# The last 64 places of a diagonal prefix sum: from one row of sums to 64 partitions under bf16 weights

## The chip, the cores and the metric

The kernel runs on one core of one Trainium2 chip. The metric is the device time of one execution in microseconds (us), taken several times; the median counts. Beside it there is a profile of one execution, whose own times are counted from its first instruction. Its engines are TensorE (PE, with the weight loads as PEld), VectorE (DVE), ScalarE (ACT), GpSimd (POOL) and SyncE (SP). SP does no arithmetic here, it only starts transfers.

## The reference

```python
def setup_inputs():
    B, H, W = 4, 4224, 4224
    return {"x": np.random.randn(B, H, W).astype(np.float32)}

def reference(x):
    ps = np.cumsum(np.cumsum(x, axis=1), axis=2)
    diag = np.diagonal(ps, axis1=1, axis2=2)
    return np.cumsum(diag, axis=1).astype(np.float32)
```

For each of four 4224 x 4224 matrices (batches), the two-dimensional prefix sum is taken along its diagonal, and the diagonal is summed up once more. The output has 4 x 4224 float32 numbers; the input has 285 MB, and every element of it is read.

## The kernel before

The places of the diagonal lie in 11 groups of 384. For each batch, strips of 768 rows are loaded (converted to bf16 by the load). TensorE counts column sums per group, VectorE and ScalarE count row sums, and two scans in VectorE turn the 11 x 384 sums into the output. The last batch (`b == 3`, not `whole`) is arranged so that little is left to do once its last rows have come in: rows 3840 to 4223 form the last group, and its last 128 rows come as four blocks of 32 rows. A block of 32 rows of 4096 columns lies on all 128 partitions, four partitions to a row, 1024 columns each; `part_b[:, s]` is block `s`. A row contributes to a place by how many places lie from that row's own place up to it, which is what the weights hold: `weights4[p, j]` counts this for partition `p` (row `p // 4` of a block) and place `j` counted from the block's first place.

The tail, which the change touches (cuts are marked `...`):

```python
    R = P // 4                                   # 32 rows of a block; P = 128
    steps = consts.tile([P, P], I32, name="steps")
    nc.gpsimd.iota(steps, pattern=[[4, P]], base=7, channel_multiplier=-1)
    ...
    weights4 = consts.tile([P, P], FP32, name="weights4")
    nc.vector.tensor_scalar_max(out=weights4, in0=steps, scalar1=0.0)
    ...
    M0 = 2 * P                                   # 256
    E0 = GW - R                                  # 384 - 32 = 352
    ...
        if not whole:
            fin_a = psum_s.tile([1, M0], FP32, name="fin_a")
            fin_b = psum_s.tile([1, P], FP32, name="fin_b")
            fin_e = psum_s.tile([1, R], FP32, name="fin_e")

        def weigh_b(rows, w, r0=0, start=False):
            matmul(fin_b[:, r0:], rows, w[..., : P - r0], start=start)
    ...
            CB = TB // 4                         # 1024 columns to a partition
            bcut = 768
            for sb, c0, c1 in ((0, 0, CB), (1, 0, CB), (2, 0, CB), (3, 0, bcut), (3, bcut, CB)):
                r0 = TB + sb * R
                nc.gpsimd.dma_start(
                    out=part_b[:, sb, c0:c1],
                    in_=x[b, r0 : r0 + R, :TB].rearrange("r (k c) -> r k c", k=4)[:, :, c0:c1],
                )
    ...
        for c in range(0, CB, P):                # block 0
            matmul(by_ps, part_b[:, 0, c : c + P], weights4_h, start=c == 0)
        ...
        act_sum(bsum[:, 0, 0:1], part_b[:, 1, :512])           # block 1: two halves
        pair_sum(bsum[:, 0, 1:2], part_b[:, 1, 512:])
        for i in (1, 0):
            weigh_b(bsum[:, 0, i : i + 1], weights4, R)
        nc.vector.tensor_add(out=yl[:, :M0], in0=fin_a, in1=last_sums[0:1, :M0])
        nc.sync.dma_start(out=out[b, T0 : T0 + M0].unsqueeze(0), in_=yl[:, :M0])
        nc.sync.dma_start(out=out[:LB, :].rearrange("b (g i) -> g b i", i=GW), in_=whole_sums)
        nc.sync.dma_start(out=out[b, :T0].rearrange("(g i) -> g i", i=GW), in_=last_sums[1:NG])
        act_sum(bsum[:, 1, 0:1], part_b[:, 2, :448])           # block 2
        pair_sum(bsum[:, 1, 1:2], part_b[:, 2, 448:])
        for i in (1, 0):
            weigh_b(bsum[:, 1, i : i + 1], weights4, 2 * R)

        act_sum(esum[:, 0:1], part_b[:, 3, :320])              # block 3
        pair_sum(esum[:, 1:2], part_b[:, 3, 320:bcut])
        pair_sum(esum[:, 2:3], part_b[:, 3, bcut:])
        nc.scalar.copy(out=yl[:, M0:], in_=fin_b)
        nc.sync.dma_start(out=out[b, T0 + M0 : T0 + E0].unsqueeze(0), in_=yl[:, M0:E0])
        for k in (1, 0, 2):
            matmul(fin_e, esum[:, k : k + 1], weights4[:, :R], start=k == 1)
        nc.vector.tensor_add(out=ye, in0=fin_e, in1=yl[:, E0:])
        nc.sync.dma_start(out=out[b, T0 + E0 : N].unsqueeze(0), in_=ye)
```

`act_sum` is a row sum on ScalarE, `pair_sum` one on VectorE that adds two halves of its input and sums the result. `matmul` loads its weights (`lhsT`) and streams `rhs`; `matmul_on` streams under the weights that are in place. Each engine runs its instructions in the order of the program, and SP too.

Of the kernel before, what the change touches and what calls it, by code (L numbers as in the profile page):

```python
# [8 lines left out]
FP32 = mybir.dt.float32  # L9
BF16 = mybir.dt.bfloat16  # L10
I32 = mybir.dt.int32
AX = mybir.AxisListType
# [5 lines left out]
def kernel(  # L18
# [14 lines left out]
    nc = tc.nc  # L33

    B, H, W = x.shape
    N = H
    P = 128
    F = 3
    F2 = 2 * F
    GW = P * F  # L40
# [3 lines left out]
    T0 = LG * GW  # L44
# [4 lines left out]
    consts = ctx.enter_context(tc.tile_pool(name="consts", bufs=1))  # L49
# [4 lines left out]
    last = ctx.enter_context(tc.tile_pool(name="last", bufs=1))  # L54
# [3 lines left out]
    psum_s = ctx.enter_context(  # L58
        tc.tile_pool(name="psum_s", bufs=1, space=bass.MemoryType.PSUM)
    )  # L60
# [61 lines left out]
    for i in range(1, NBUF):  # L122
# [5 lines left out]
        out=um1,  # L128
        in_=um1,
        compare_op=ALU.is_gt,  # L130
        fill=0.0,
        base=0,
        pattern=[[1, GW]],
        channel_multiplier=-1,
# [5 lines left out]
        out=ident,  # L140
        in_=ident,
        compare_op=ALU.is_equal,
        fill=0.0,
        base=0,
        pattern=[[-1, P]],
        channel_multiplier=1,
# [27 lines left out]
    def between_groups(name, turned):  # L174
# [27 lines left out]
        out=weights,  # L202
        in_=weights,
        compare_op=ALU.is_ge,
        fill=0.0,
        base=0,
        pattern=[[1, GW]],
        channel_multiplier=-1,
# [1 line left out]


    R = P // 4
    steps = consts.tile([P, P], I32, name="steps")
    nc.gpsimd.iota(steps, pattern=[[4, P]], base=7, channel_multiplier=-1)
    nc.vector.tensor_single_scalar(
        out=steps, in_=steps, scalar=2, op=ALU.arith_shift_right
    )
    weights4 = consts.tile([P, P], FP32, name="weights4")
    nc.vector.tensor_scalar_max(out=weights4, in0=steps, scalar1=0.0)

    ident_h = consts.tile([P, P], BF16, name="ident_h")
    nc.vector.tensor_copy(out=ident_h, in_=ident)
# [1 line left out]
    def matmul(o, lhsT, rhs, start=False):  # L224
        nc.tensor.matmul(  # L225
            o, lhsT=lhsT, rhs=rhs, start=start, stop=False, skip_group_check=True
        )

    def matmul_on(o, lhsT, rhs):

        te = nc.tensor
        te.add_instruction(  # L232
            mybir.InstMatmult(
                start_tensor_calc=False,
                stop_tensor_calc=False,
                tile_position=(0, 0),
                tile_size=(P, P if lhsT.shape[-1] > 64 else 32),
                bass_skip_group_check=True,
                ldweights=False,
                name=nc.get_next_instruction_name(),  # L240
                engine=te.engine,
                ins=[
                    te.lower_ap(rhs, opt=False),
                    te.lower_ap(lhsT, opt=False, for_matmul_weights=True),
                ],
                outs=[te.lower_ap(o)],
            )
        )

    weights4_h = consts.tile([P, P], BF16, name="weights4_h")  # L250
    nc.vector.tensor_copy(out=weights4_h, in_=weights4)
    ones_col = consts.tile([P, 1], FP32, name="ones_col")
    nc.vector.memset(ones_col, 1.0)

    def fold_in(o, src, c0, c1, w, start=False):

        for c in range(c0, c1, w):
            e = min(c + w, c1)
            if c == c0:
                matmul(o[..., : e - c], ident_h, src[..., c:e], start=start)  # L260
            else:
                matmul_on(o[..., : e - c], ident_h, src[..., c:e])

    def act_sum(acc, src):
        w = src.shape[-1]
        dump = dumpool.tile([P, 2176], BF16, name="dump")
        nc.scalar.activation(  # L267
            out=dump[:, :w], in_=src, func=ACT.Copy, accum_out=acc
        )
# [6 lines left out]
    def pair_sum(acc, src):  # L276

        w = src.shape[-1] // 2
        if not pairs:
            pairs.append(last.tile([P, 288], FP32, name="pair"))  # L280
        pair = pairs[0]
        nc.vector.scalar_tensor_tensor(
            out=pair[:, :w],
            in0=src[:, :w],
            scalar=1.0,
            in1=src[:, w:],
            op0=ALU.mult,
            op1=ALU.add,
            accum_out=acc,
        )  # L290
# [37 lines left out]
    last_sums = last.tile([NG, GW], FP32, name="last_sums")  # L328

    M0 = 2 * P  # L330
    E0 = GW - R

    for b in range(B):
        whole = b < LB
# [9 lines left out]
        def row_of(j):  # L344
            return (j + t0) % NG

        if not whole:
            fin_a = psum_s.tile([1, M0], FP32, name="fin_a")
            fin_b = psum_s.tile([1, P], FP32, name="fin_b")
            fin_e = psum_s.tile([1, R], FP32, name="fin_e")  # L350

        def weigh_b(rows, w, r0=0, start=False):

            matmul(fin_b[:, r0:], rows, w[..., : P - r0], start=start)
# [8 lines left out]
        def columns(j, lo, hi, rhs, same=False):  # L363


            k = row_of(j)
            lhsT = sel[:, NG - 1 - k : 2 * NG - 1 - k]
            if same:
                matmul_on(d[:, lo:hi], lhsT, rhs)
                return  # L370
            matmul(d[:, lo:hi], lhsT, rhs, start=first[0])
            first[0] = False
# [65 lines left out]
        for h in range(2):  # L438
            ps = slice(h * HP, (h + 1) * HP)
            k = row_of(h)  # L440
            nc.vector.tensor_copy(
                out=r6[ps, k : k + 2 * ns : 2, :], in_=a6[ps, :, :, 1]
# [24 lines left out]
        if not whole:  # L467
# [3 lines left out]
            part_b = strip[:, 2, :TB].rearrange("p (s c) -> p s c", s=4)  # L471
# [3 lines left out]
            CB = TB // 4  # L475
            bcut = 768
            for sb, c0, c1 in (
# [8 lines left out]
                    out=part_b[:, sb, c0:c1],  # L486
                    in_=x[b, r0 : r0 + R, :TB].rearrange("r (k c) -> r k c", k=4)[
                        :, :, c0:c1
                    ],
# [29 lines left out]
        for i, (to, src) in enumerate(((c1, d), (c2, c1))):  # L519
            nc.vector.tensor_tensor_scan(  # L520
                out=to,
# [8 lines left out]


        yl = last.tile([1, GW], FP32, name="yl")
        ye = last.tile([1, R], FP32, name="ye")
        c0, c1 = acuts[1]
        fold_in(fold_a, part_a, c0, c1, 256)
        by_ps = psum_s.tile([P, P], FP32, name="fold")
# [9 lines left out]


        bsum = last.tile([P, 2, 2], FP32, name="bsum")
        esum = last.tile([P, 3], FP32, name="esum")
        act_sum(bsum[:, 0, 0:1], part_b[:, 1, :512])  # L550
        pair_sum(bsum[:, 0, 1:2], part_b[:, 1, 512:])
        for i in (1, 0):
            weigh_b(bsum[:, 0, i : i + 1], weights4, R)
        nc.vector.tensor_add(out=yl[:, :M0], in0=fin_a, in1=last_sums[0:1, :M0])
        nc.sync.dma_start(
            out=out[b, T0 : T0 + M0].unsqueeze(0), in_=yl[:, :M0]
        )
        nc.sync.dma_start(
            out=out[:LB, :].rearrange("b (g i) -> g b i", i=GW), in_=whole_sums
        )  # L560
        nc.sync.dma_start(
            out=out[b, :T0].rearrange("(g i) -> g i", i=GW), in_=last_sums[1:NG]
        )
        act_sum(bsum[:, 1, 0:1], part_b[:, 2, :448])
        pair_sum(bsum[:, 1, 1:2], part_b[:, 2, 448:])
        for i in (1, 0):
            weigh_b(bsum[:, 1, i : i + 1], weights4, 2 * R)


        act_sum(esum[:, 0:1], part_b[:, 3, :320])  # L570
        pair_sum(esum[:, 1:2], part_b[:, 3, 320:bcut])
        pair_sum(esum[:, 2:3], part_b[:, 3, bcut:])
        nc.scalar.copy(out=yl[:, M0:], in_=fin_b)
        nc.sync.dma_start(
            out=out[b, T0 + M0 : T0 + E0].unsqueeze(0), in_=yl[:, M0:E0]
        )
        for k in (1, 0, 2):
            matmul(fin_e, esum[:, k : k + 1], weights4[:, :R], start=k == 1)
        nc.vector.tensor_add(out=ye, in0=fin_e, in1=yl[:, E0:])
        nc.sync.dma_start(out=out[b, T0 + E0 : N].unsqueeze(0), in_=ye)  # L580


# [28 lines left out]
```

## Time and profile before

| what | value |
|---|---|
| median of 3 runs | 667.94 us (667.25 to 668.96) |
| profiled execution: time, span | 667.23 us, 665.5 us |
| VectorE busy | 380.3 us, 57% of the span |
| TensorE busy | 206.7 us, 31% |
| ScalarE busy | 136.8 us, 21% |
| DMA | 143.23 MB written, mean 215 GB/s |
| HBM read over the span | 285.47 MB, 429 GB/s |

The span is the time from the first to the last instruction; the rest of the measured time lies outside it. Busy shares are averages over the whole span; the change sits in the last 5 us or so, so the timeline and the waits of that stretch say more than the shares. In a timeline line the columns are start, duration, engine, line of the program, operation, output and inputs with their shapes, count, and in brackets the idle time before it with what ended it. A stretch of fp32 matmuls is counted in passes: one fp32 matmul shows as two.

### The profile page before, as it was taken

What the parts mean: (1) busy time and instruction counts of PE and PEld (TensorE: products, weight loads), DVE (VectorE), ACT (ScalarE), POOL (GpSimd) and SP (SyncE); (2) the same over time, 40 slices, a digit from 0 to 9 for tenths busy, and PEclk for the clock granted to TensorE, in tenths of its full rate; (3) what the DMA queues carried; (4) which work ended last, traced back from release to release, by engine and by line L of the source; (5) the groups of instructions that cost most, each with busy time, mean ns of one, the idle gap of its engine ahead of it and who ended that gap; (6) DMA issues with size and microseconds to landing.
All of it is one profiled execution on the core that took longest, in us unless ns stands there. A gap on an engine that the chain in (4) does not pass through costs nothing.

```text
span 665.5 us, 2519 instructions
## 1 busy us (share of the span) xinstructions
PE 206.7 (31%) x956; PEld 94.5 (14%) x956; DVE 380.3 (57%) x174; ACT 136.8 (21%) x223; POOL 31.7 (5%) x60
## 2 busy tenths in 40 slices
PE   0071522302117143140311723404021354450428
PEld 0030211100003021010000311201000121220103
DVE  4161828476946173756794526557589433362866
ACT  0001120406300103040630020304063002030434
POOL 4300000000000000000000000000000000001000
PEclk9995857656559585665655857657565595875758
DMA  9999999999999999999999999999999999999998
GB/s 203 219 219 219 219 218 218 215 207 216 219 221 218 218 220 217 218 215 210 216 219 220 216 219 218 219 216 214 215 216 218 217 218 218 218 216 219 214 207 165
DMA packets 7666, 143.23 MB, mean 215 GB/s; under 512 B 698, under 2 KB 998, under 8 KB 2150
## 3 DMA queue, kind: packets, MB, share of 16 engines
q0 software_dynamic: 7312, 142.47, 100.0%
q1 hardware_dynamic: 342, 0.61, 0.4%
q8 instruction: 7, 0.11, 0.1%
q14 instruction: 5, 0.04, 0.0%
HBM read 285.47 MB, written 0.07 MB: 429 GB/s over the span
## 4 chain that ended last, share of the span: by engine, by line
DVE 50%; another core or an unknown queue 32%; DMA 15%; POOL 1%; PE 1%; issue 1%; DVEq 0%; POOLq 0%
DVE acc L272 26%; DMA strip<-in_x_dram 14%; DVE rowed L272 7%; DVE mu L387 7%; DVE strip L388 7%; PE d L225 1%; POOL um L107 1%; DMA head<-in_x_dram 1%; DVE um L106 1%; DVE c L520 0%; DVE whole_sums L520 0%; POOL strip L485 0%; DVE pu L272 0%; DVE whole_sums L293 0%
## 5 line engine op out<-in xcount | busy, mean ns | idle before, releaser
L267 ACT ACTIVATE dump<-strip 128x416 bf16<-128x416 bf16 (+6 forms) x108 | 124.4, 1152 | 519.7 <-DMA strip<-in_x_dram 517.0
L387 DVE TENSOR_TENSOR mu<-strip,um 128x4608 bf16<-128x4608 bf16 (+1 forms) x24 | 52.4, 2184 | 254.9 <-DMA strip<-in_x_dram 254.8
L272 DVE TENSOR_REDUCE acc<-strip 128x6 f32<-128x4608 bf16 (+6 forms) x23 | 195.9, 8519 | 0.4
L232 PEld LDWEIGHTS <-sel 128*11 128x11 bf16 x643 | 66.4, 103 | 475.8 <-issue 446.5
L225 PE MATMUL d<-strip,sel 128*11 128x384 bf16 x90 | 37.1, 412 | 280.5 <-DMA strip<-in_x_dram 280.5
L232 PE MATMUL d<-strip,sel 128*11 128x384 bf16 x441 | 116.0, 406 | 13.9 <-DMA strip<-in_x_dram 13.9
L388 DVE TENSOR_TENSOR strip<-strip,mu 128x4608 bf16<-128x4608 bf16 (+1 forms) x24 | 52.4, 2183 | 1.0
L225 PE MATMUL d<-mu,sel 128*11 128x384 bf16 x43 | 16.3, 379 | 108.4 <-DVE mu L387 108.4
L272 DVE TENSOR_REDUCE rowed<-strip 128x384 f32<-128x2304 bf16 x12 | 48.9, 4074 | 0.0
L232 PE MATMUL d<-mu,sel 128*11 128x384 bf16 x200 | 46.3, 366 | 0.0
L76 POOL DMA_DIRECT2D strip<-in_x_dram x23 | 15.6, 680 | 535.3 <-DVE acc L272 293.2
L267 ACT ACTIVATION_READ_ACCUMULATOR dump<-strip 128x1 f32 x108 | 20.1, 186 | 0.0
L225 PE MATMUL d<-rowed,sel_f 128*11 128x384 f32 x24 | 11.7, 576 | 20.9 <-DVE rowed L272 20.9
L225 PEld LDWEIGHTS <-sel 128*11 128x11 bf16 x134 | 13.6, 101 | 23.2 <-issue 11.2
L225 PE MATMUL d<-ident,rows 128*11 128x128 f32 x24 | 5.2, 379 | 16.8 <-DVE rows L450 16.8
L272 DVE TENSOR_REDUCE pu<-d 11x1 f32<-11x384 f32 x4 | 2.2, 546 | 6.2 <-PE d L225 6.2
L107 POOL TENSOR_SCALAR_AFFINE_SELECT um<-um 128x4608 bf16<-128x4608 bf16 (+1 forms) x2 | 5.2, 2622 | 8.7 <-DVE um L106 8.7
L106 DVE MEMSET um<- 128x4608 bf16 (+1 forms) x2 | 4.9, 2458 | 1.1 <-issue 1.1
L225 PE MATMUL d<-halves,rows 128*11 128x64 f32 x48 | 5.3, 289 | 0.0
L225 PEld LDWEIGHTS d<-ident,rows 128*11 128x11 f32 x24 | 2.5, 119 | 18.9 <-DVE rows L450 11.7
L225 PEld LDWEIGHTS d<-rowed,sel_f 128*11 128x11 f32 x24 | 1.5, 92 | 25.4 <-DVE rowed L272 25.1
L225 PEld LDWEIGHTS d<-halves,rows 128*11 128x11 f32 x48 | 4.8, 129 | 1.3 <-issue 1.1
(110 smaller groups left out, 64.6 us busy)
## 6 DMA issues: line engine op xcount, KB each, us to landing
strip<-in_x_dram POOLq DMA_DIRECT2D x18, 6336.0 KB, 72.8
strip<-in_x_dram POOLq DMA_DIRECT2D x7, 3168.0 KB, 55.8
strip<-in_x_dram POOLq DMA_DIRECT2D x1, 1080.0 KB, 49.9
strip<-in_x_dram POOLq DMA_DIRECT2D x1, 768.0 KB, 52.9
strip<-in_x_dram POOLq DMA_DIRECT2D x3, 256.0 KB, 54.1
head<-in_x_dram SPq DMA_DIRECT2D x1, 528.0 KB, 3.9
strip<-in_x_dram POOLq DMA_DIRECT2D x1, 192.0 KB, 43.2
strip<-in_x_dram POOLq DMA_DIRECT2D x1, 64.0 KB, 28.6
```

What stands on the lines that cost most here:

```text
L76: nc.gpsimd.dma_start(out=o, in_=x[b, r0 : r0 + f * P, :].rearrange("(p f) w -> p f w", f=f))
L106: nc.vector.memset(um, 1.0)
L107: nc.gpsimd.affine_select(out=um, in_=um, compare_op=ALU.is_gt, fill=0.0, base=0, pattern=[[-1, f], [1, f * P]], channel_multiplier=-f,)
L225: nc.tensor.matmul(o, lhsT=lhsT, rhs=rhs, start=start, stop=False, skip_group_check=True)
L232: te.add_instruction(mybir.InstMatmult(start_tensor_calc=False, stop_tensor_calc=False, tile_position=(0, 0), tile_size=(P, P if lhsT.shap ...
L267: nc.scalar.activation(out=dump[:, :w], in_=src, func=ACT.Copy, accum_out=acc)
L272: nc.vector.reduce_sum(out=acc, in_=src, axis=AX.X)
L387: nc.vector.tensor_mul(out=mu, in0=block, in1=um)
L388: nc.vector.tensor_sub(out=block, in0=block, in1=mu)
```

## The change

It widens the last piece from 32 to 64 places and turns it onto partitions. Before, block 3 is summed along its columns by ScalarE and VectorE, and the sums are then weighted by TensorE into a row of 32 places on one partition. After, TensorE streams block 3 itself, in eight pieces of 128 columns, under bf16 weights (64 of them per partition, one per place) into a PSUM tile of 64 partitions x 128 columns; VectorE then sums along the columns, so that the sum over columns comes after the weights and in one instruction. Column 129 of that tile holds what the 64 places get from elsewhere: the rows up to block 1 (turned from a row onto partitions by a matmul with a single one), and block 2. The weights get 32 more columns in front, in which block 3 counts nothing for block 2's places. The first 320 places leave in one store instead of two, and the last 64 in a store whose 64 pieces have 4 bytes each, one from each partition. It is meant to shorten the work between the landing of the last rows and the last store.

```diff
-    steps = consts.tile([P, P], I32, name="steps")
-    nc.gpsimd.iota(steps, pattern=[[4, P]], base=7, channel_multiplier=-1)
+    steps = consts.tile([P, R + P], I32, name="steps")
+    nc.gpsimd.iota(steps, pattern=[[4, R + P]], base=7 - 4 * R, channel_multiplier=-1)
 ...
-    weights4 = consts.tile([P, P], FP32, name="weights4")
-    nc.vector.tensor_scalar_max(out=weights4, in0=steps, scalar1=0.0)
+    weights4_w = consts.tile([P, R + P], FP32, name="weights4_w")
+    nc.vector.tensor_scalar_max(out=weights4_w, in0=steps, scalar1=0.0)
+    weights4 = weights4_w[:, R:]
 ...
-    weights4_h = consts.tile([P, P], BF16, name="weights4_h")
-    nc.vector.tensor_copy(out=weights4_h, in_=weights4)
+    weights4_hw = consts.tile([P, R + P], BF16, name="weights4_hw")
+    nc.vector.tensor_copy(out=weights4_hw, in_=weights4_w)
+    weights4_h = weights4_hw[:, R:]
 ...
-    E0 = GW - R
+    S = 2 * R
+    E0 = GW - S
 ...
-            fin_e = psum_s.tile([1, R], FP32, name="fin_e")
+            fin_e = psum_s.tile([S, P + 1], FP32, name="fin_e")
 ...
-        ye = last.tile([1, R], FP32, name="ye")
+        ye = last.tile([S, 1], FP32, name="ye")
 ...
         nc.vector.tensor_add(out=yl[:, :M0], in0=fin_a, in1=last_sums[0:1, :M0])
         nc.sync.dma_start(
-            out=out[b, T0 : T0 + M0].unsqueeze(0), in_=yl[:, :M0]
-        )
-        nc.sync.dma_start(
             out=out[:LB, :].rearrange("b (g i) -> g b i", i=GW), in_=whole_sums
         )
 ...
         act_sum(bsum[:, 1, 0:1], part_b[:, 2, :448])
         pair_sum(bsum[:, 1, 1:2], part_b[:, 2, 448:])
+        nc.vector.tensor_copy(out=yl[:, M0:], in_=fin_b)
+        nc.sync.dma_start(
+            out=out[b, T0 : T0 + E0].unsqueeze(0), in_=yl[:, :E0]
+        )
+
+        matmul(fin_e[:, P:], yl[:, E0:], ones_col[0:1], start=True)
         for i in (1, 0):
-            weigh_b(bsum[:, 1, i : i + 1], weights4, 2 * R)
-
-        act_sum(esum[:, 0:1], part_b[:, 3, :320])
-        pair_sum(esum[:, 1:2], part_b[:, 3, 320:bcut])
-        pair_sum(esum[:, 2:3], part_b[:, 3, bcut:])
-        nc.scalar.copy(out=yl[:, M0:], in_=fin_b)
-        nc.sync.dma_start(
-            out=out[b, T0 + M0 : T0 + E0].unsqueeze(0), in_=yl[:, M0:E0]
-        )
-        for k in (1, 0, 2):
-            matmul(fin_e, esum[:, k : k + 1], weights4[:, :R], start=k == 1)
-        nc.vector.tensor_add(out=ye, in0=fin_e, in1=yl[:, E0:])
-        nc.sync.dma_start(out=out[b, T0 + E0 : N].unsqueeze(0), in_=ye)
+            matmul(fin_e[:, P:], weights4[:, :S], bsum[:, 1, i : i + 1])
+        for c in range(0, CB, P):
+            piece = part_b[:, 3, c : c + P]
+            if c == 0:
+                matmul(fin_e[:, :P], weights4_hw[:, :S], piece, start=True)
+            else:
+                matmul_on(fin_e[:, :P], weights4_hw[:, :S], piece)
+        nc.vector.reduce_sum(out=ye, in_=fin_e, axis=AX.X)
+        nc.sync.dma_start(out=out[b, T0 + E0 : N].unsqueeze(1), in_=ye)
```

More of the change, by code (lines that the diff above doesn't have):

```diff
@@ L236, in matmul_on @@
                 tile_position=(0, 0),
-                tile_size=(P, P if lhsT.shape[-1] > 64 else 32),
+                tile_size=(P, P if lhsT.shape[-1] > 64 else 64 if lhsT.shape[-1] > 32 else 32),
                 bass_skip_group_check=True,
@@ L548 @@
         bsum = last.tile([P, 2, 2], FP32, name="bsum")
-        esum = last.tile([P, 3], FP32, name="esum")
         act_sum(bsum[:, 0, 0:1], part_b[:, 1, :512])
```

## The prediction

> **What bounds the kernel now.** I read the page first, for what fills the span, then the chain that ended last, then the timeline of the last 4 us, and then what SP waits for. On the page, the DMA row shows the 16 DMA engines busy in every slice, and the queue of the loads alone fills them:
>
> ```profile
> DMA  9999999999999999999999999999999999999998
> ...
> q0 software_dynamic: 7312, 142.47, 100.0%
> q1 hardware_dynamic: 342, 0.61, 0.4%
> ```
>
> So the loads set some 662 of the 665.5 us, and nothing in the change makes them fewer. What can move is the tail behind them, and anything that gets in among them. The chain, in order of time (start, duration, what):
>
> ```profile
> 618.94 43.22 DMA strip<-in_x_dram
> ...
> 662.25 0.29 DVE pair L282
> ...
> 662.71 0.57 PE fin_e L225 x6
> ...
> 663.36 0.18 DVE ye L579
> ```
>
> The loads end it until 662.16, then VectorE, TensorE and VectorE follow. The trace's completion records tell the landings apart: block 1 at 659.99, block 2 at 661.22, the first 768 columns of block 3 at 662.16, its last 256 at 662.50 (a transfer is whole at its sixteenth completion). The timeline around them:
>
> ```profile
> 661.32 0.46 DVE L282 SCALAR_TENSOR_TENSOR pair<-strip 128x288 f32<-128x288 bf16 x1
> 661.32 0.98 PE L225 MATMUL fin_b<-weights,bsum 128*1 128x96 f32 x8
> ...
> 662.68 0.29 DVE L282 SCALAR_TENSOR_TENSOR pair<-strip 128x128 f32<-128x128 bf16 x1
> ...
> 662.71 0.55 PE L225 MATMUL fin_e<-weights,esum 128*1 128x32 f32 x6 [0.40 <-DVE pair L282]
> ...
> 663.36 0.18 DVE L579 TENSOR_TENSOR ye<-fin_e,yl 1x32 f32<-1x32 f32 x1 [0.38 <-PE fin_e L225]
> 663.57 0.23 SPq L580 DMA_DIRECT2D out_dram<-ye  x1
> ```
>
> From the last landing (662.50) to the last store's issue (663.57) pass 1.07 us: that is all the arithmetic that the change can shorten. Its packet starts at 664.27, its completion comes at 664.60, 1.03 us after issue, and 0.9 us of closing follow. The last view is SP's waits:
>
> ```profile
> SPq L555 <- DVE yl L554: 660.0, 1, 660.0
> ```
>
> SP starts the head's load at 0.82 us and then stands for 660 us before the first store of `yl`. The two big stores behind it (`whole_sums` 49.5 KB, `last_sums` 15.0 KB) have long been ready: they wait only for SP's order.
>
> **What the Trainium skill says.** "TensorE: Matmul & The Clock Gate", section "LDWEIGHTS (loading the stationary operand)", lets a weight load's time grow with its columns, columns / 1.2 ns: 53 ns for 64, an estimate. No weight load before has 64 columns; those of one column take 79 to 84 ns each, overlapped. "VectorE: DVE Perf Modes", section "The perf-mode tier table (the rule you actually need)", says a reduce handles one element per cycle whatever the type; the trace agrees (11x384 fp32 from PSUM in 546 ns, 128x480 in 650 ns: 1.08 ns a column). "DMA: Bandwidth & Descriptors", section "Issuing engines are not separate DMA queues", says that transfers of all issuing engines share the same 16 DMA engines and interleave, and section "Why a DMA increments its semaphore by 16 and not by 1" that the size of the slowest dimension sets how many engines a store uses. The trace agrees: the `whole_sums` store of 11 partitions completes in 11 steps after a first jump, that of `last_sums` with 10 in 10.
>
> **The change part by part.**
>
> *Removed.* On ScalarE 0.47 + 0.19 us for block 3 and the 0.24 us copy, on VectorE the two sums of block 3 (0.39 + 0.08 and 0.29 + 0.08), on TensorE six passes of 32 columns, and the first `yl` store. On the path are one VectorE sum, TensorE and the add.
>
> *The new chain on TensorE.* In program order, the matmuls over block 3 now stand behind a matmul that needs `yl`, so behind VectorE's copy of `fin_b`. VectorE is done with block 2 at 661.79 (accumulator read 661.70 + 0.08), and the last of the four block-1 passes into `fin_b` starts at 661.57 and takes 0.246, so 661.82. With 0.07 us for the signal the copy starts at 661.89. Its length from two VectorE instructions on one partition, 1x256 in 0.412 and 1x32 in 0.179, is 1.04 ns a column, so 0.28 for 128: done at 662.17, TensorE goes on at about 662.20. Then six fp32 passes with 64-column weights and one streamed column; at about 0.06 us each (the 53 ns above, and a little) 0.36: 662.56. By then both parts of block 3 are there. The eight bf16 matmuls of 128 columns are those of block 0, which took 0.62 us in all (658.77 to 659.39; the granted clock is 1.00 from 655 on). With 0.05 for the first weights they end at 663.23. VectorE starts 0.10 later (before: 663.26 to 663.36), and the reduce of 129 columns takes 0.546 - 255 x 0.00108 = 0.27: 663.60. With 0.03 to SP the store is issued at 663.63, against 663.57 before: +0.06.
>
> If the fp32 passes go faster than this, the landing at 662.50 binds instead: two matmuls behind it (0.05 + 0.06 + 0.22) end at 662.83, and 0.10 + 0.27 + 0.03 put the issue at 663.23, -0.34. That needs TensorE to be through 3a by 662.55, so to be free of the fp32 passes at 662.2, which I believe only in part. I take -0.05.
>
> *The store in 64 pieces.* One piece before: 0.70 us from issue to its packet, then 0.33 to completion. The head's load with its 256 pieces shows its first packet 1.07 us after issue, so (1.07 - 0.70) / 255 = 1.5 ns a piece, 0.09 for 64. Four pieces and a completion on each of 16 engines, at some 20 ns each (the 384-byte packet of `yl` took 20), add 0.08, and the slowest of sixteen engines counts instead of one. I put +0.2 on it.
>
> *Stores that move.* With the first `yl` store gone, SP comes to `whole_sums` at once and issues it when its third scan is done (the scan starts at 520.2 and takes 1.0), and `last_sums` after its second scan at 659.66. Both then run in the middle of a full load stream, where before they ran after it, in the shadow of the tail (their last completion 663.93). 64.5 KB of 1024 bytes are 66 kB; at the 429 GB/s of the page that is 0.15 us, which delays the last landing and everything behind it. At the 215 GB/s of the written side it would be 0.31. I take +0.15.
>
> *At the start* the weights are 160 columns wide instead of 128; three strips of loads are in the queue then, nothing waits for it: 0.
>
> Sum: -0.05 + 0.2 + 0.15 = +0.3 us, the span 665.8 instead of 665.5. On the median of 667.94 that is 668.2 us.
>
> **The rivals.** (a) *TensorE gets through early*, and the chain ends 0.34 earlier; with stores that cost nothing the time is 667.6. For it speaks that the one-column passes are short and the array's clock is full; against it, that two VectorE-to-TensorE handovers stand in its way at 661.8 to 662.2. (b) *The 4-byte pieces are dear*: all 64 land within 256 bytes of HBM, and if their writes go one after another at, say, 20 ns each, the store is 1.3 us longer and the time 669.3. Nothing before has such a store; the completions of 4 bytes (9 ns each) go to semaphores, and prove nothing for HBM. (c) *The moved stores cost nothing or twice as much*: they use 11 and 10 of 16 engines, and only the engines that finish last count. The sixteen completions of the last load spread from 661.17 to 662.50, six of them within 0.1 us of the end, so it can be 0 or 0.3: 668.1 or 668.4.
>
> **Range and chances.** All of these lie within about -0.4 to +1.5 us of the old time. The three runs before spread by 1.7 us, which is more than my step; so the range is mainly that scatter around 668.2: 667.2 to 669.2. Two per cent are 13 us, over four times the 3.0 us from the last landing to the end of the span; nothing here reaches it. Chances: faster by over 2% 0.005, within 2% 0.99, slower by over 2% 0.005.
>
> **What would show it.** `whole_sums` should be issued near 521 us and `last_sums` near 659.7. The copy into `yl` should end before 662.2, the six fp32 passes near 662.6, the reduce take 0.27, and the last store be issued at about 663.6 after a landing at about 662.65. From that issue to its completion should pass 1.2 us. I am wrong if the weight loads of 64 fp32 columns take far from 0.06 us each, if the store of 64 pieces completes in under 1.1 or over 1.6 us, or if the last landing moves by over half a microsecond.

## The result

The changed kernel takes 674.08 us (median of 5 runs, 673.45 to 674.89) against 667.78 us before (5 runs, 667.25 to 668.96). The ratio is 1.009, with a 95% interval of 1.0075 to 1.0105: slower by 6.3 us. The prediction put it at 668.2 us with a range of 667.2 to 669.2. That nothing here would reach two per cent holds, but by luck: it was argued from the 3.0 us between the last landing and the end of the span, and these have become 9.55 us (663.60 to 673.15). The loss is twenty times the step that was predicted, and lies outside the range.

The page of the profile after, with the DMA row and the queues:

```profile
DMA  9999999999999999999999999999999999999993
...
q0 software_dynamic: 7312, 142.47, 98.8%
q1 hardware_dynamic: 418, 0.61, 0.3%
```

The loads are the same packets. The last digit of the DMA row has gone from 8 to 3, and the small queue has 76 packets more: at the end there is a stretch without traffic. What SP waits for, in the profile after (engine, line, what it waited for, us in total, times, longest):

```profile
SPq L557 <- DVE acc L411: 520.5, 1, 520.5
...
SPq L607 <- DMA out_dram<-ye: 6.0, 1, 6.0
SPq L566 <- DVE yl L565: 2.2, 1, 2.2
```

and the last of these in the profile before:

```profile
SPq L606 <- DMA out_dram<-ye: 0.3, 1, 0.3
```

That is the loss. At the end of the program SP waits 6.0 us for the last store, where it waited 0.3. The first line shows that `whole_sums` is no longer held up until 661 us: SP comes to it at once and stands only until its scan is done (the scan ends at 521.65, the store is issued at 521.69; `acc` is what VectorE writes right behind it). The tail's timeline after the change (start, duration, engine, line, operation; idle time before it in brackets):

```profile
663.48 0.28 DVE L565 COPY yl<-fin_b 1x128 f32<-1x128 f32 x1 [0.20 <-PE fin_b L226]
...
663.82 0.27 PE L226 MATMUL fin_e<-ones_col,yl 1*64 1x1 f32 x2 [0.37 <-DVE yl L565]
...
664.02 0.39 PE L226 MATMUL fin_e<-bsum,weights_w 128*64 128x1 f32 x4
...
664.33 0.55 PE L233 MATMUL fin_e<-strip,weights_hw 128*64 128x128 bf16 x7
664.92 0.28 DVE L580 TENSOR_REDUCE ye<-fin_e 64x1 f32<-64x129 f32 x1 [1.16 <-PE fin_e L233]
665.23 0.54 SPq L581 DMA_DIRECT2D out_dram<-ye  x1
```

The new arithmetic is short, as planned, but it starts late: from the last landing (663.60) to the issue pass 1.63 us, where it was 1.07. After the issue at 665.23 nothing computes any more; the table of stretches (length, busy time of PE, PEld, DVE, ACT and POOL with counts, clock, DMA share, GB/s) says so in one line:

```profile
666.00:673.20 7.20, 0.00 (x0) 0.00 (x0) 0.00 (x0) 0.00 (x0) 0.00 (x0) 0.73 0.01 0
```

By the trace's records, the 64 packets of 4 bytes and their sixteen completions have all left the DMA engines by 1.36 us after the issue, each in 7 to 9 ns. But the completions arrive in a staircase from 2.07 to 7.01 us after it. Before, the one packet of 128 bytes was complete after 1.03 us. The two profiled executions lie 7.66 us apart (674.89 and 667.23 us; the profiled one was the longest of the five after). Of these the store accounts for 5.98, the later landing (663.60 instead of 662.50) for 1.10, and the way from landing to issue for 0.56. What it is about this store that costs so much was open.

### The profile page after: what moved, and what is told of

The parts are those of the page before. It is cut to its first block, busy times and chain, and to the rows that moved or that the text cites. A ratio compares the mean times of both kernels' runs of the same rounds, so it can differ in the third digit from the quotient of the medians.

```text
span 673.2 us, 2516 instructions
## 1 busy us (share of the span) xinstructions
PE 207.6 (31%) x960; PEld 95.9 (14%) x960; DVE 379.8 (56%) x171; ACT 136.2 (20%) x220; POOL 31.7 (5%) x60
## 4 chain that ended last, share of the span: by engine, by line
DVE 52%; another core or an unknown queue 34%; DMA 8%; PE 3%; issue 1%; POOL 1%; DVEq 0%
DVE acc L274 27%; DMA strip<-in_x_dram 7%; DVE mu L390 7%; DVE strip L391 7%; DVE rowed L274 7%; PE d L226 1%; DVE c L523 1%; POOL um L107 1%; DMA head<-in_x_dram 1%; DVE um L106 1%; DVE whole_sums L523 0%; PE fold L233 0%; PE d L233 0%; DVE pu L274 0%
```

## The experiments

Theories. **Sharing**: writes of 4 bytes wait for each other because they fall into the same few bytes of HBM. **Pieces**: a small piece, or a descriptor, costs this much wherever it lands. **Source**: 64 partitions or sixteen engines on the SBUF side cost it. **Moved stores** and **chain**: the loss comes from the stores that now run among the loads, or from the new arithmetic, and the late completion is only where it shows. Times of a run are compared with the kernel before on the same chip.

### The 64 numbers in one piece

```diff
         nc.vector.reduce_sum(out=ye, in_=fin_e, axis=AX.X)
-        nc.sync.dma_start(out=out[b, T0 + E0 : N].unsqueeze(1), in_=ye)
+        matmul(fin_r, ye, ident[:S, :S], start=True)     # back onto one partition
+        nc.vector.tensor_copy(out=yr, in_=fin_r)
+        nc.sync.dma_start(out=out[b, T0 + E0 : N].unsqueeze(0), in_=yr)
```

> The changed kernel, but its 64 sums are turned back onto one partition by a matmul with the identity and a copy, and leave in one piece of 256 bytes. If the store of 64 pieces is the cost (7.0 us from issue to completion in the profile after, against 1.0 before), the store's completion comes about 1.0 us after its issue, some 0.6 us are added for matmul and copy, and the time is 674.1 - 6.0 + 0.6 = 668.7 us, within 1.5 us of the kernel before. If the moved stores or the new chain on TensorE are the cost, it stays at 672 to 675 us.

Measured: 668.22 us, before 667.32; ratio 1.0015 (1.0008 to 1.0022). Its store completes 1.06 us after issue. Its tail:

```profile
663.70 0.28 DVE L580 TENSOR_REDUCE ye<-fin_e 64x1 f32<-64x129 f32 x1 [1.16 <-PE fin_e L233]
664.03 0.27 PE L226 MATMUL fin_a<-ident,ye 64*1 64x64 f32 x2 [0.38 <-DVE ye L580]
664.34 0.21 DVE L584 COPY yr<-fin_a 1x64 f32<-1x64 f32 x1 [0.36 <-PE fin_a L226]
664.58 0.23 SPq L585 DMA_DIRECT2D out_dram<-yr  x1
```

From the end of the reduce (663.98) to the issue, the way back takes 0.60 us. With all the rest of the change in place, its moved stores and its chain, 0.90 us of the 6.30 remain, and 0.60 of these are the way back. The loss is the form of the last store; chain and moved stores together can hold only a few tenths.

### The first store of `yl` back in its place

```diff
+        nc.sync.dma_start(out=out[b, T0 : T0 + M0].unsqueeze(0), in_=yl[:, :M0])
         nc.sync.dma_start(out=out[:LB, :].rearrange("b (g i) -> g b i", i=GW), in_=whole_sums)
 ...
-            out=out[b, T0 : T0 + E0].unsqueeze(0), in_=yl[:, :E0]
+            out=out[b, T0 + M0 : T0 + E0].unsqueeze(0), in_=yl[:, M0:E0]
```

> The changed kernel with the first store of yl put back in its place, so that the whole_sums and last_sums stores wait for it again and run after the loads. If the moved stores are the cost, the time falls to about 668 us. If the store of 64 pieces is, it stays within 0.5 us of 674.1 us, and the last landing comes 0.15 us or so earlier, which scatter hides.

Measured: 673.69 us, before 667.32; ratio 1.0097 (1.0082 to 1.0112). The big stores run in the tail again, and nothing is won: 6.37 us over the kernel before, against 6.30. The last store completes 6.92 us after issue.

### The moved stores alone

```diff
-        nc.sync.dma_start(out=out[b, T0 : T0 + M0].unsqueeze(0), in_=yl[:, :M0])
 ...
-            out=out[b, T0 + M0 : T0 + E0].unsqueeze(0), in_=yl[:, M0:E0]
+            out=out[b, T0 : T0 + E0].unsqueeze(0), in_=yl[:, :E0]
```

> The kernel before with one edit: the first store of yl is left out and its 256 numbers leave with the later one, so that the whole_sums store runs near 521 us and the last_sums store near 660 us, among the loads. If stores among the loads cost what the prediction put on them, the time rises by 0.15 to 0.3 us; if they cost nothing, by less than 0.1 us.

Measured: 667.43 us, before 667.28; ratio 1.0004 (0.9995 to 1.0012). The difference of 0.15 us is the size predicted, but the interval reaches from -0.3 to +0.8 us, so it can't be told from nothing. The last landing in its profile, 662.54, is that of the kernel before (662.50).

### 32 small pieces from one partition

```diff
-        ye = last.tile([1, R], FP32, name="ye")
+        ye2 = last.tile([1, R, 2], FP32, name="ye2")
+        ye = ye2[:, :, 0]
```

> The kernel before, but the 32 numbers of its last store lie 8 bytes apart on their one partition, so that they leave in 32 pieces of 4 bytes; all else as before. If pieces of 4 bytes into neighbouring addresses cost about 6.0 / 64 = 0.09 us each, the store takes 1.0 + 2.9 us and the time is about 670.7 us. If the cost comes from 64 partitions or sixteen engines on the source side, it stays near 667.8 us.

Measured: 669.74 us, before 667.32; ratio 1.0037 (1.0024 to 1.0050), so +2.4 us, somewhat less than the 2.9 expected. The store completes after 3.33 us instead of 1.03, which is 0.07 us a piece; 0.54 of it is the first packet, which starts 1.24 us after the issue instead of 0.70. The source is one partition: **source**, as 64 partitions, is out. The sixteen engines are not, since the 32 pieces leave through sixteen (sixteen completions) and the one piece before through one.

### Two series of stores

After the changed kernel's end, stores of a constant tile go to a scratch tensor one by one; VectorE may refill the tile only when the store before has completed. `RUNGS` stands for the list in each of the two texts below; each series was executed once.

```diff
 ...
+        def rung(rows, width, step):
+            nc.vector.memset(tl, 1.0)
+            nc.sync.dma_start(
+                out=scr[: rows * step].rearrange("(r c) -> r c", c=step)[:, :width],
+                in_=tl[:rows, :width])
+        for rows, width, step in RUNGS:
+            rung(rows, width, step)
```

> The changed kernel, and after its last store a series of stores of a constant tile into a scratch tensor in HBM, each started when the one before has completed; the output is that of the changed kernel, the time is longer by the series. Rungs, as pieces x bytes at distance: 1x256; 64x4 at 4, 64, 256, 512 and 4096 bytes; 64x64 at 64; 64x512 at 512; 16x4, 32x4 and 61x4 at 4; then seven of them again. If writes into the same line of memory wait for each other, 64x4 at 4 takes about 7 us, 16x4 and 32x4 about 2.5 and 4, and 64x4 at 512 and 4096 bytes 1.2 us. If each small piece costs the same wherever it lands, all of 64x4 take 7 us. If only the number of pieces matters, 64x64 and 64x512 take 7 us too.

> The changed kernel with a second series of stores after it, each started when the one before has completed. Rungs, as pieces x bytes at distance: 1x256; 8x4, 16x4, 16x4, 24x4, 32x4, 48x4, 64x4 at 4; 64x4 at 8, 16, 32 and 64; 64x8 at 8, 64x16 at 16, 64x32 at 32; 61x4 at 4 and at 64 (61 goes to one engine); 32x4 at 8, 32 and 64. If writes into one 64-byte line wait for each other, the time per rung falls with the pieces per line and not with the pieces: 64x4 at 8, 16, 32 and 64 about 7, 4, 2 and 2 us, 64x32 at 32 about 2 us, and 61x4 at 64 about 2 us against 8.6 at 4. If one engine's second small piece is what costs, 61x4 at 64 stays near 8.6 us, and 24x4 (two to an engine) is as slow as 32x4 while 16x4 is not.

The refills of the first series behind 1 x 256 bytes, 64 x 4 side by side, and 64 x 4 at 64 bytes (in brackets, how long VectorE waited for the store):

```profile
701.39 0.17 DVE L587 MEMSET tl<- 128x128 f32 x1 [1.22 <-DMA scratch<-tl]
707.99 0.17 DVE L587 MEMSET tl<- 128x128 f32 x1 [6.43 <-DMA scratch<-tl]
709.96 0.17 DVE L587 MEMSET tl<- 128x128 f32 x1 [1.81 <-DMA scratch<-tl]
```

and of the second, behind 64 x 4 bytes at 8, at 16 and at 32 bytes:

```profile
700.81 0.17 DVE L587 MEMSET tl<- 128x128 f32 x1 [3.87 <-DMA scratch<-tl]
703.64 0.17 DVE L587 MEMSET tl<- 128x128 f32 x1 [2.67 <-DMA scratch<-tl]
705.60 0.17 DVE L587 MEMSET tl<- 128x128 f32 x1 [1.79 <-DMA scratch<-tl]
```

Same tile, same 64 pieces of 4 bytes, same sixteen engines; only the distance differs, and at 32 bytes the wait is gone. From the trace's records, us from issue to the last completion (rungs that ran beside the program's own last store are left out):

| pieces x bytes | side by side | at 8 bytes | at 16 | at 32 | at 64 | at 256 to 4096 |
|---|---|---|---|---|---|---|
| 64 x 4 | 6.25, 7.65 | 3.69 | 2.49 | 1.62 | 1.63 | 1.62 to 1.65 |
| 48 x 4 | 7.20 | | | | | |
| 32 x 4 | 4.50, 4.68 | 3.19 | | 1.29 | 1.28 | |
| 24 x 4 | 2.79 | | | | | |
| 16 x 4 | 1.28, 1.52 | | | | | |
| 61 x 4 (one engine) | 7.37, 8.25 | | | | 1.75 | |
| 64 x 8 | 3.73 | | | | | |
| 64 x 16 | 1.93 | | | | | |
| 64 x 32 | 1.62 | | | | | |
| 64 x 64 | 1.62 | | | | | |
| 64 x 512 | 1.75 | | | | | |
| 1 x 256 | 1.04 | | | | | |

**Pieces** is out: 64 of them, 32 bytes or more apart, cost 0.6 us more than one piece, not 6. **Sharing** holds, and its unit is finer than the 64 bytes that I had put: two pieces within 64 bytes cost nothing when 32 apart, two within 32 bytes (64 x 4 at 16) cost 0.87 us in all. The bound lies somewhere between 16 bytes (which cost) and 32 (which don't), and no series moved the start of the pieces; that the unit is a fixed stretch of 32 bytes is inferred. Where one engine sends everything (61 pieces), the cost is about the same, and at 64 bytes it goes away too, so the number of an engine's own pieces isn't the cause. With that, and with 64 pieces through sixteen engines that cost only 0.6 us at 32 bytes, **source** is out as sixteen engines too. Pieces of 32 bytes side by side are free of it.

### Four stores of sixteen pieces

```diff
-        nc.sync.dma_start(out=out[b, T0 + E0 : N].unsqueeze(1), in_=ye)
+        for i in range(4):
+            nc.sync.dma_start(
+                out=out[b, T0 + E0 + 16 * i : T0 + E0 + 16 * i + 16].unsqueeze(1),
+                in_=ye[16 * i : 16 * i + 16])
```

> The changed kernel with its last store cut into four stores of 16 pieces of 4 bytes, each to 64 bytes of its own. In the series before, 16 pieces (one to an engine) completed 0.5 us later than one piece of 256 bytes, 32 and 64 pieces 3.4 and 5.2 us later. If what costs is a second small piece of the same engine, or more than 16 pieces in one store, the four stores overlap and the time is about 674.1 - 6.0 + 1.3 = 669.4 us. If the 64 writes wait for each other because they land within 256 bytes, whoever issues them, it stays within 1 us of 674 us.

Measured: 675.68 us (673.92 to 681.42), before 667.28; ratio 1.0141 (1.0103 to 1.0179). The median is 1.7 us above 674, more than the 1 us allowed for, in four runs that scatter by 7.5; it is nowhere near 669.4. In its profiled execution TensorE ran at about half its pace in the tail (the four passes into `fin_a` took 1.52 us, 0.81 in the profile after), so I read only the store from it (it is the one of 681.42 us; the other three took 673.92 to 676.85). From the first issue to the last completion pass 7.55 us. The first sixteen complete together, within 1.29 us of their issue; those of the other three come mostly in steps of 0.40 us, three at a time. So a store of sixteen can slip through, but four of them don't: the limit isn't a count within one store. A second piece of the same engine is not excluded by this run, since each store gives every engine one more; the 61 pieces above exclude it.

### The same store, far and close, in the kernel

```diff
+        scr = nc.dram_tensor("scratch", [16 * S], FP32, kind="Internal").ap()
-        nc.sync.dma_start(out=out[b, T0 + E0 : N].unsqueeze(1), in_=ye)
+        nc.sync.dma_start(out=scr.rearrange("(r c) -> r c", c=16)[:, 0:1], in_=ye)
```

For the close one, `[S]` and `c=1`. Both leave out the last 64 places of the output.

> The changed kernel, but its 64 last pieces of 4 bytes go to a scratch tensor in HBM, 64 bytes apart (the last 64 places of the output are left out). In the series of stores such a store completed 1.62 us after its issue, the same pieces side by side after 6.2 to 7.7. If that sharing of 32 bytes is the whole loss, the time is 674.1 - 5.4 = 668.7 us, and what stays above the kernel before (667.3 to 667.8) is the new chain and the store's longer issue, about 1 us. If the output tensor or the chain matters, it is elsewhere.

> As the run with pieces 64 bytes apart, but side by side in the scratch tensor (256 bytes in all), the last 64 places of the output left out: the same number, size and target tensor, only the distance differs. If the distance is what counts, 673.5 to 674.5 us, 5.4 us above it.

Measured: 64 bytes apart 668.43 us, ratio 1.0015 (1.0006 to 1.0023); side by side 673.93 us, ratio 1.0096 (1.0081 to 1.0111); before 667.33 for both. The wait at the program's end, far:

```profile
SPq L610 <- DMA scratch<-ye: 0.7, 1, 0.7
```

and close:

```profile
SPq L610 <- DMA scratch<-ye: 6.0, 1, 6.0
```

The distance in the access pattern is worth 5.50 us, and the scratch tensor behaves as the output does. That is the cause, shown in the kernel itself.

### A version with two pieces

```diff
+        ye32 = last.tile([S, R], FP32, name="ye32")      # ye is its first column
+        yt = last.tile([S, R], FP32, name="yt")
 ...
         nc.vector.reduce_sum(out=ye, in_=fin_e, axis=AX.X)
+        nc.vector.transpose(out=yt, in_=ye32)            # 32x32 blocks
-        nc.sync.dma_start(out=out[b, T0 + E0 : N].unsqueeze(1), in_=ye)
+        nc.sync.dma_start(
+            out=out[b, T0 + E0 : N].rearrange("(h i) -> h i", i=R), in_=yt[0:S:R, :])
```

Further, the first `yl` store is back, and TensorE streams the first six pieces of block 3 before block 2's sums and `yl`, the last two after them.

> The changed kernel with the first store of yl put back; TensorE streams the first six pieces of block 3 as soon as they land and takes block 2 and yl between them and the last two pieces; after the reduce VectorE transposes 32x32 blocks (64x32), so that the 64 numbers lie on two partitions and leave in two pieces of 128 bytes. If the small pieces were the whole loss, the time is 667.8 us or less: issue of the last store 0.05 + 0.28 + 0.10 + 0.28 + 0.15 + 0.03 = 0.9 us after the last landing, against 1.07 before, so -0.2 us at best. If something else in the new chain costs, it stays above 669 us.

Measured: 668.31 us, before 667.28; ratio 1.0015 (1.0009 to 1.0022). It lies 1.03 us above the kernel before, where the change lies 6.30 above it: better than the change by 5.3 us, and no gain over the kernel before. Its tail:

```profile
662.34 0.22 PE L226 MATMUL fin_e<-strip,weights_hw 128*64 128x128 bf16 x1 [0.65 <-DMA strip<-in_x_dram]
...
662.67 0.34 PE L226 MATMUL fin_e<-bsum,weights_w 128*64 128x1 f32 x4
...
663.48 0.28 DVE L587 TENSOR_REDUCE ye<-fin_e 64x1 f32<-64x129 f32 x1 [1.39 <-PE fin_e L233]
663.80 0.20 DVE L588 STREAM_TRANSPOSE yt<-ye 64x32 f32<-64x32 f32 x1
664.03 0.58 SPq L589 DMA_DIRECT2D out_dram<-yt  x1
```

The last landing is at 662.63; the issue comes 1.40 us later, not 0.9. The six fp32 passes now stand between the two parts of block 3: TensorE turns to them at 662.67, just as the last part lands, and comes to that part at 663.14. The store of two pieces takes 0.58 us to issue (0.23 before) and completes after 1.55 us (1.03). That makes 0.33 + 0.52, and with the landing's 0.13 the 1.0 us by which it is slower.

## Why the prediction was wrong

- **The store in 64 pieces, "I put +0.2 on it": this is the step that failed.** It measured +5.98 us in the two profiles (7.01 against 1.03), far beyond the 1.6 us that the prediction named as a sign of being wrong. I priced the way to the packets and their number. That part came out too low as well: the first packet starts 1.18 us after the issue where I had 0.79 (0.70 + 0.09), and 64 pieces at 32 bytes or more complete in 1.62, about +0.6 where I had +0.2. But what I left out is the large part. I left the writes' own way in HBM to rival (b), at "say, 20 ns each", and gave it no weight, since the kernel before had no such store to read it from. The kind of cause in (b), writes close together that wait for each other, is the one found. Its size is 5.50 / 64 = 0.086 us a piece between the far and the close store, and 0.07 to 0.11 in the series for 32, 61 and 64 pieces (each less the same pieces 64 bytes apart), about four times what (b) assumed.
- **The new chain, -0.05 against the landing**, did not come out in the profile after: from the landing to the issue pass 1.63 us instead of 1.07; in the other five profiles with this chain and its store, 0.96 to 1.36. Its length was right: from the start of the copy of `fin_b` to the issue pass 1.75 us (663.48 to 665.23) in this and in each of the five, predicted 1.74 (661.89 to 663.63). Its terms: copy 0.28 (predicted 0.28), six fp32 passes with 64-column weights 0.45 (0.36), reduce 0.28 (0.27). The weight loads of 64 fp32 columns last 136 ns each but start some 55 ns apart (four in the 0.22 us from 664.02 to 664.24), which agrees with the 53 ns estimated from the Trainium skill, "TensorE: Matmul & The Clock Gate", section "LDWEIGHTS (loading the stationary operand)"; the two passes over `yl`, whose next start comes 0.20 us after their own, took the rest. What was wrong is the start at 661.89, which I had from a single profile; see below.
- **The landing** came at 663.60 instead of 662.50, where the prediction had 662.65. The loads were late before the tail began: TensorE's first matmul over the strip before it starts at 649.71 instead of 648.66. The runs with other stores landed between 662.54 and 663.14, with the big stores early or late; one profile of each can't say what this rests on, and it stays open.
- **The moved stores, +0.15**: that they would move was right (`whole_sums` at 521.69 us, predicted 521; `last_sums`, predicted near 659.7, only at 661.32, behind its late scan). Their price measured 0.15 with an interval of -0.3 to +0.8, so it is neither confirmed nor refuted.
- **The sum**, from the runs: the store side by side in the scratch tensor lies 6.60 us above the kernel before, the change itself 6.30 (5.0 to 7.0). Of the 6.60, 5.50 are the sharing (close less far). Of the other 1.10, 0.63 are 64 pieces instead of one (1.66 - 1.03, from issue to completion); some 0.5 are left for the chain, the moved stores and the scatter of the landing.
- **The range** followed the scatter of the runs, as if the terms were known that well. A term for which no view of the profile had an example should have widened it: rival (b) was named at +1.3 us and then shut out by a range that ended at 669.2. With (b) let in it would still have missed 674.1: the size of (b) was a guess that no number of the profile bounded.

Why the chain started late can be read from TensorE. The copy starts 3.20 us after the last scan of `last_sums` (660.28 in the profile after; before, 658.65, and 658.65 + 3.20 = 661.85 is about what I predicted). TensorE's work leads up to that scan, and in the stretches ahead of it TensorE is busy without a break in both profiles, but at different granted clocks (the third number from the right). Before:

```profile
652.00:654.00 2.00, 2.00 (x14) 1.07 (x14) 2.00 (x2) 1.49 (x2) 0.00 (x0) 0.65 1.07 213
654.00:656.00 2.00, 2.00 (x19) 1.07 (x16) 0.38 (x2) 0.00 (x0) 0.00 (x0) 1.00 1.09 217
```

and after:

```profile
652.00:654.00 2.00, 2.00 (x7) 0.60 (x6) 2.00 (x1) 1.97 (x3) 0.00 (x0) 0.50 1.06 211
654.00:656.00 2.00, 2.00 (x16) 1.36 (x14) 1.43 (x3) 0.54 (x2) 0.00 (x0) 0.59 1.07 213
```

The clock goes from 0.50 to 1.00 at 653.4 before and at 655.6 after. Over the eleven profiles in which it is recorded, a scan start of 658.3 to 658.7 goes with a rise at 651.7 to 653.4, one of 659.0 to 659.5 with a rise at 654.0 to 654.7, and 660.28 with 655.6. Kernels with the changed tail stand in all three groups, so nothing here puts the late rise down to the change; and no run set the clock, so that it made the scan late is argued from this order.

The Trainium skill, "DMA: Bandwidth & Descriptors", section "Specifications", says that transfers below 512 bytes make the engine read, change and write back. Size alone does not explain what was measured: 4 bytes at a distance of 32 complete in 1.62 us, the same as 32 bytes side by side. It is small pieces less than 32 bytes apart that wait.

Left open: what makes them wait, and where. Completions come in steps of 0.40 us in the four stores, but sixteen pieces in 64 bytes, alone or as the first of the four stores, got through in 1.3 to 1.5 us though they lie as close, and the cost grows with pieces and sharers in no simple proportion (64 x 4 at 16, at 8 and side by side add 0.87, 2.07 and 4.6 to 6.0 us). No run told the DMA engines' write path from the memory's.

## What to carry to other kernels

A last store is paid to its completion, not to its last packet: look at the wait for it at the program's end, and at when its completions arrive. Don't let many small pieces of one store, or of stores in flight together, land within the same 32 bytes of HBM; a result that lies one number to a partition is cheaper turned back onto one partition (0.60 us here) than stored as it lies (some 6 us for 64 numbers). And where a change brings a kind of transfer that the profile has no example of, the range must at least let in the worst rival, however small the bytes; here even that would have been too narrow, so such a transfer is better measured alone first.

## What was not expected of the hardware

- 64 pieces of 4 bytes side by side take 6.2 to 7.7 us to complete, and 1.62 us when 32 bytes apart; in the series their packets have left the DMA engines after 1.28 or 1.29 us either way.
- One engine alone pays the same: 61 pieces side by side 7.4 to 8.3 us, 64 bytes apart 1.75.
- A store of two pieces of 128 bytes from partitions 0 and 32 took 0.58 us to issue and 1.55 to complete; one piece of 256 bytes takes 0.23 and 1.06.
- The full clock of TensorE began anywhere between 651.7 and 655.6 us in eleven profiles of nearly the same work up to there.
